# Sums of squares for the norm of k: the block of ones held in the array and the squares' exact halves streamed, 512 tokens at a time, then laid out through memory

## The chip, the cores and the metric

The kernel is one program on one core of one Trainium2 chip. A core has five engines that run at their own pace and wait for one another through semaphores: TensorE (PE in the rows; PEld is its weight load, which runs beside the matmul before it), VectorE (DVE), ScalarE (ACT), GpSimd (POOL) and SyncE (SP), which here only issues DMA transfers. Each engine takes its instructions strictly in the order in which they stand, DMA issues included (SPq and ACTq in the rows). A matmul has a stationary operand, loaded into the array first, and a moving operand that is streamed through it; its result goes to PSUM, and ACT or DVE copies it from there to SBUF.

The metric is the device time of the whole program in microseconds (us). Three runs of the kernel before took 3341.09, 3333.39 and 3338.21 us, so the median is 3338.21 us.

## The reference, cut to what matters

One layer of a bidirectional encoder: a combined projection, a bidirectional RWKV-7 scan (8 heads of 64, 2048 tokens), windowed attention, and a mixture of experts. The change touches one quantity, the norm of `kk` per head and token:

```python
k = u[..., 512:1024]                                  # columns of the projection, token-shifted
kk = heads(k * k_k)                                   # (2048 tokens, 8 heads, 64)
kk = kk / max(sqrt(sum(kk * kk, axis=-1)), 1e-12)     # one norm per head and token
...
wkv += wkv7_scan(r, decay, kd, v, -kk, kk * a, reverse)
```

So 8 x 2048 sums of 64 squares are wanted, and their inverse square roots are multiplied into `kk` before the scan reads it.

## The kernel before, in words

A scheduler orders the instructions of each engine when the program is built: the source is written stage by stage, and the scheduler interleaves what is ready by its own estimate of durations. The order is fixed from then on. Where a buffer (a named tile in a pool) is used again, the new user waits for the last reader of the old one; pools that are opened later take the same SBUF space as pools that were closed, and their first users wait for the last users of that space.

Four stages matter here.

**Norm and transposes (0 to about 72 us).** x is normalised and transposed into `hq[q]`, four quarters of 512 tokens each, as two parts whose sum is the exact value (`float32r`, a form that TensorE takes in one pass; plain float32 takes it two records of a matmul and of a weight load for each call).

**Projection in columns (about 37 to 397 us).** A loop takes 14 blocks `c` of 128 columns of w_in in the order 4, 5, 6, 7, 12, 13, 0, 1, 2, 3, 8, 9, 10, 11; blocks 4 to 7 are k, two heads each. For each block and each quarter, 24 matmuls (8 pieces of the inner dimension, 3 products of parts; L280) sum into one PSUM bank `pp` of 3, and ACT copies it to `u` (L283). So a block is 96 matmuls of 128x128 stationary and 512 moving columns. Then ACT scales `u` (L285) and DVE adds the two neighbour tokens (L286, L287) into `dst` (tile `m`, or `xwa` for block 12).

For a block of k, ACT squares `dst`, scaled by k_k, into `u` (L292), and 16 matmuls in plain float32 (L295) take 128 tokens each: the squares are stationary, `blk` (128x2, ones in the rows of one head per column) moves. Each leaves 128 tokens x 2 heads in one PSUM tile `ssq`, so tokens lie on partitions. After block 7, DVE takes the maximum with 1e-24 and the inverse square root (L316 and the helper at L104 to L109), PE transposes the result (L320), DVE copies it out (L322), and SP writes it to memory as `inv_d`, 8 heads x 2048 tokens (L323). From there ACT's queue reads it back, spread over 64 partitions (L265), in 16 pieces: `normalise` loads a piece of k (L262), multiplies (L267) and writes it (L268). The pieces are spread over blocks 13, 0, 1 and 2.

**Start of the scan (about 397 to 600 us).** SP loads 14 small parameter rows into `qrow` (buffer `Zs`, L346 to L350), the two up-projections `upw` (L353, L354), the v rows `uv` that blocks 8 to 11 wrote to memory (L304, L399) and the r, k, kk slices `ld` (L427). PE transposes `qrow` (L377). Then `prep` runs four times: matmuls (L436), tanh, a chain of DVE, ACT and POOL operations, transposes (L484), products (L493). `invert` follows, mainly on DVE, and then 64 steps of the scan.

**Filler.** The rest of the projection (attention columns and gates, "dense", L716 and L720; its weights come through L656, L658, L659) is a generator that is drawn in fixed numbers of steps between the pieces of `prep`, `invert` and the scan steps. The scheduler may move it further.

The lines that the sums rest on:

```python
S.activation(u[:, 0:T], dst, AF.Square, scale=P[:, 44 + pr:45 + pr])
for i in range(NT):
    o = ssq[:, :128].rearrange("p (h i) -> p h i", h=H)[:, 2 * pr:2 * pr + 2, i]
    PE.matmul(o, u[:, i * 128:(i + 1) * 128], blk, start=True, stop=True)
```

## Time and profile before

| | |
|---|---|
| runs | 3341.09, 3333.39, 3338.21 us; median 3338.21 us |
| the profiled execution's own time | 3351.28 us |
| its span, first to last instruction | 3349.6 us |
| PE busy | 3024.1 us, 90% of the span |
| DVE busy | 2210.9 us, 66% |
| ACT busy | 1522.0 us, 45% |
| mean granted TensorE clock | 0.957 of full speed |

How to read it. The profile comes from one execution. "Idle before" names what ended the idle time of an engine. A matmul's duration covers its whole way through the array, and the next one starts before it ends; what a matmul costs in a dense run is the distance from one start to the next, which is read from a stretch and its count. A `clock` of 1.00 is the level of 2.4 GHz and 0.50 that of 1.2 GHz; between them lies a stretch that had both.

### The profile page before, as it was taken

What the parts mean: (1) busy time and instruction counts of PE and PEld (TensorE: products, weight loads), DVE (VectorE), ACT (ScalarE), POOL (GpSimd) and SP (SyncE); (2) the same over time, 40 slices, a digit from 0 to 9 for tenths busy, and PEclk for the clock granted to TensorE, in tenths of its full rate; (3) what the DMA queues carried; (4) which work ended last, traced back from release to release, by engine and by line L of the source; (5) the groups of instructions that cost most, each with busy time, mean ns of one, the idle gap of its engine ahead of it and who ended that gap; (6) DMA issues with size and microseconds to landing.
All of it is one profiled execution on the core that took longest, in us unless ns stands there. A gap on an engine that the chain in (4) does not pass through costs nothing. (4 is left out here: it accounts for less than half of the span.)

```text
span 3349.6 us, 72079 instructions
## 1 busy us (share of the span) xinstructions
PE 3024.1 (90%) x29102; PEld 2466.8 (74%) x29102; DVE 2210.9 (66%) x4134; ACT 1522.0 (45%) x2913; POOL 544.8 (16%) x648
## 2 busy tenths in 40 slices
PE   6999978888989998898999987999996999999997
PEld 4888777667877787678877886778784667777775
DVE  5233368566766686648664776677774677888885
ACT  6333344453434434343433864111122566677764
POOL 0000012011112020112110000323233121222231
PEclk9899989999999999999999999999996999999999
DMA  7144365666545655565456654444433899999986
GB/s 280 60 136 137 98 208 194 211 199 206 161 150 174 201 167 160 166 199 162 145 172 184 182 174 144 129 130 144 127 120 115 286 308 323 337 336 341 330 295 201
DMA packets 361082, 652.63 MB, mean 195 GB/s; under 512 B 33717, under 2 KB 181765, under 8 KB 356522
## 3 DMA queue, kind: packets, MB, share of 16 engines
q1 hardware_dynamic: 338538, 599.61, 53.8%
q0 software_dynamic: 11104, 36.32, 4.4%
q10 hardware_dynamic: 11104, 12.06, 1.1%
q8 instruction: 230, 3.77, 0.5%
q14 instruction: 106, 0.87, 0.1%
HBM read 497.52 MB, written 153.10 MB: 194 GB/s over the span
## 5 line engine op out<-in xcount | busy, mean ns | idle before, releaser
L716 PE MATMUL dn<-wh,hk 128*128 128x256 f32 x3456 | 475.4, 295 | 24.0 <-DVE wh L659 9.4
L1289 DVE TENSOR_TENSOR wh<-raw,wh 128x1024 fp32r<-128x1024 f32 x376 | 441.4, 1219 | 80.1 <-ACT wh L1288 79.1
L716 PEld LDWEIGHTS dn<-wh,hk 128*128 128x128 f32 x3456 | 443.8, 200 | 42.5 <-DVE wh L659 11.1
L1288 ACT ACTIVATE wh<-raw 128x1024 fp32r<-128x1024 f32 x384 | 387.3, 1053 | 149.9 <-DMA raw<-in_w_down_dram 69.2
L720 PE MATMUL dn<-hk,wh 128*128 128x512 f32 x1536 | 404.1, 411 | 30.6 <-ACT gs L730 11.0
L1418 PE MATMUL pgu<-wh,xT 128*128 128x512 f32 x1536 | 377.7, 403 | 0.2 <-ACT xT L1393 0.2
L720 PEld LDWEIGHTS dn<-hk,wh 128*128 128x128 f32 x1536 | 284.5, 193 | 106.9 <-ACT gs L730 13.2
L1418 PEld LDWEIGHTS pgu<-wh,xT 128*128 128x128 f32 x1536 | 287.9, 190 | 78.1 <-issue 7.4
L280 PE MATMUL pp<-hq,wh 128*128 128x512 f32 x1008 | 254.0, 408 | 1.6 <-ACT hq L217 1.3
L280 PEld LDWEIGHTS pp<-hq,wh 128*128 128x128 f32 x1008 | 193.1, 194 | 48.0 <-ACT hq L217 2.3
L1174 PE MATMUL px<-w,mT 128*128 128x512 f32 x768 | 196.2, 406 | 0.0
L1462 PE MATMUL py<-wh,hT 128*128 128x512 f32 x768 | 191.4, 401 | 0.4 <-ACT hT L1440 0.4
L476 POOL TENSOR_TENSOR t<-t,ld 128x512 f32<-128x512 f32 x32 | 51.2, 1600 | 857.6 <-DVE t L465 483.9
L1174 PEld LDWEIGHTS px<-w,mT 128*128 128x128 f32 x768 | 142.8, 188 | 36.8 <-issue 3.4
L1462 PEld LDWEIGHTS py<-wh,hT 128*128 128x128 f32 x768 | 140.4, 188 | 33.1 <-issue 1.2
L1354 POOL DMA_INDIRECT out_dram<-ys,IDX x49 | 91.2, 1861 | 315.5 <-issue 105.5
L283 ACT ACTIVATE u<-pp 128x512 f32<-128x512 f32 x56 | 61.3, 1094 | 152.3 <-PE pp L280 125.3
L730 ACT ACTIVATE gs<-dn,drv 128x512 f32<-128x512 f32 x64 | 75.7, 1183 | 116.9 <-PE dn L720 80.5
L1158 PE MATMUL ab<-yT,w 128*128 128x256 f32 x768 | 114.4, 293 | 7.2 <-DVE tg L1161 3.6
L1378 POOL DMA_INDIRECT xg<-h_d,IDX x49 | 72.7, 1484 | 280.2 <-PE tx L1392 175.1
L1158 PEld LDWEIGHTS ab<-yT,w 128*128 128x128 f32 x768 | 99.5, 193 | 12.4 <-DVE tg L1161 5.6
L415 ACT ACTIVATE uv<-pre 32x512 f32<-32x512 f32 x128 | 75.2, 588 | 61.1 <-PE pre L409 59.9
(415 smaller groups left out, 5434.5 us busy)
## 6 DMA issues: line engine op xcount, KB each, us to landing
wh<-wc_d SPq DMA_DIRECT2D x204, 512.0 KB
raw<-in_w_gate_dram SPq DMA_DIRECT2D x64, 1024.0 KB
raw<-in_w_up_dram SPq DMA_DIRECT2D x64, 1024.0 KB
raw<-in_w_down_dram SPq DMA_DIRECT2D x64, 1024.0 KB
wc_d<-wh SPq DMA_DIRECT2D x68, 512.0 KB
ld<-rkk_d SPq DMA_DIRECT2D x192, 128.0 KB
raw<-in_w_in_dram SPq DMA_DIRECT2D x82, 256.0 KB
g_d<-gs SPq DMA_DIRECT2D x64, 256.0 KB
```

Of the source, the lines that this page charges most:

```text
L280: PE.matmul(pp, whs[k // 4][:, a, k % 4], hq[q][k // 2][:, k % 2, b], start=n == 0, stop=n == 3 * KT - 1)
L415: S.activation(uv[p * 64:p * 64 + 32, s::2].rearrange("p s (h e n) -> p s h e n", e=2, n=N)[:, :, :, e], pa[o:o + 32], AF.Copy)
L716: PE.matmul(pp[e][:, j * 256:(j + 1) * 256], lhs(2 * e + j, hk, k, a), wk_[:, b], start=k + j + m == 0, stop=k + j + m == KT + 2, skip_gro ...
L720: PE.matmul(pp[e], wk_[:, a, e * 128:e * 128 + 128], hk[k // 2][:, k % 2, b], start=k + m == 0, stop=k + m == KT + 1)
L730: S.activation(natural(gs), by_residue(pp[e]), AF.Tanh, scale=0.5, bias=DP[:, 38 + ct:39 + ct])
L1158: PE.matmul(pa[:, e], wt[k][:, a, cs_], src[:, k, b], start=e + n == 0, stop=n == 3 * nk - 1, skip_group_check=True)
L1174: PE.matmul(px, mT[k // 4][:, k % 4, a, j * 128:(j + 1) * 128], wO[k][:, b, fs], start=n == 0, stop=n == 3 * KT - 1)
L1288: S.activation(wh[:, 0, ks], raw[:, ks], AF.Copy)
L1289: eng.tensor_tensor(wh[:, 1, ks], raw[:, ks], wh[:, 0, ks], op=OP.subtract)
L1354: G.indirect_dma_start(out=x2_d, out_offset=bass.IndirectOffsetOnAxis(ap=idx, axis=0), in_=src, in_offset=None, bounds_check=T - 1, oob_is ...
L1418: PE.matmul(pgu[n], xT[:, x_, 4 * a + k], wh[:, w_, k], start=a + k + m == 0, stop=a + k + m == 6)
L1462: PE.matmul(py[f], hT[:, x_, 2 * a + k], wh[:, w_, k, f * 512:(f + 1) * 512], start=a + k + m == 0, stop=a + k + m == 4)
```

## The change

For each block of k, the squares in `u` are taken 512 tokens at a time. ACT copies them to `float32r` (the first half, `sh[:, 0]`), DVE subtracts that from the squares (the second half, `sh[:, 1]`; the two add up to the squares), and two matmuls sum both halves with `blkr`, the ones in `float32r`, as stationary operand (128x2): 2 partitions x 512 tokens in PSUM. ACT copies that to `sums` (2x2048), and SP writes `sums` to a new memory tensor `ss_d`, 8 x 2048. After block 7, SP reads `ss_d` back as 128 partitions x 128 tokens, DVE makes the inverse square roots in place of before, and SP writes them to `inv_d` as they lie; the transpose and the copy after it are gone. The pool `up` gets `blkr`, `sh` (two buffers of 4 KB a partition) and `sums` (8 KB), and loses `ivT`.

```diff
+    ss_d = scratch("ss_d", [H, T])
...
-        ssq = mk(ps1, [128, 512], F32, "ssq", bufs=1)
+        blkr = mk(up, [128, 2], F32R, "blkr")
+        S.activation(blkr, blk, AF.Copy)
...
                 S.activation(u[:, 0:T], dst, AF.Square, scale=P[:, 44 + pr:45 + pr])
-                for i in range(NT):
-                    o = ssq[:, :128].rearrange("p (h i) -> p h i", h=H)[:, 2 * pr:2 * pr + 2, i]
-                    PE.matmul(o, u[:, i * 128:(i + 1) * 128], blk, start=True, stop=True)
+
+                sums = mk(up, [2, T], F32, "sums")
+                for i4 in range(4):
+                    ts_ = slice(i4 * 512, (i4 + 1) * 512)
+                    sh = mk(up, [128, 2, 512], F32R, "sh", bufs=2)
+                    S.activation(sh[:, 0], u[:, ts_], AF.Copy)
+                    V.tensor_tensor(sh[:, 1], u[:, ts_], sh[:, 0], op=OP.subtract)
+                    pt = mk(ps1, [128, 512], F32, "ssq", bufs=1)
+                    for b in range(2):
+                        PE.matmul(pt[0:2], blkr, sh[:, b], start=b == 0, stop=b == 1)
+                    S.activation(sums[:, ts_], pt[0:2], AF.Copy)
+                nc.sync.dma_start(ss_d[2 * pr:2 * pr + 2], sums)
...
-                V.tensor_scalar(sv, ssq[:, :128], 1e-24, None, op0=OP.max)
+                nc.sync.dma_start(sv, ss_d.rearrange("h (i p) -> (h i) p", p=128))
+                V.tensor_scalar(sv, sv, 1e-24, None, op0=OP.max)
                 iv = mk(up, [128, 128], F32, "iv")
                 rsqrt(up, iv, sv, [128, 128], "rk")
-                pt = mk(ps1, [128, 512], F32, "tp")
-                PE.transpose(pt[:, :128], iv, ident)
-                ivT = mk(up, [128, 128], F32, "ivT")
-                V.tensor_copy(ivT, pt[:, :128])
-                nc.sync.dma_start(inv_d.rearrange("h (i p) -> (h i) p", p=128), ivT)
+                nc.sync.dma_start(inv_d.rearrange("h (i p) -> (h i) p", p=128), iv)
```

The scheduler's order changes at these places. From the projection's line on, lines of the kernel after stand 2 to 8 higher than those of before (L280 is now L282, L377 is L385, L436 is L444, L716 is L724).

PE before, in the second quarter of block 7 (`pp_1028`): the 16 matmuls for block 6's squares (`u_856`) stand in one piece.

```order
L280 MATMUL pp_1028<-hq_24_106,wh_152_996 128x512 x6
L280 MATMUL pp_1028<-hq_25_107,wh_152_996 128x512 x2
L295 MATMUL ssq_577<-blk_78,u_856 128x2 x16
L280 MATMUL pp_1028<-hq_25_107,wh_152_996 128x512 x4
L280 MATMUL pp_1054<-hq_26_108,wh_150_991 128x512 x6
```

PE after, the same place (second quarter `pp_1072`, third `pp_1098`): the eight matmuls for block 6 (L304) stand apart, a pair for each 512 tokens.

```order
L282 MATMUL pp_1072<-hq_26_108,wh_180_1040 128x512 x5
L304 MATMUL ssq_1003<-sh_1000,blkr_578 2x512
L282 MATMUL pp_1072<-hq_26_108,wh_180_1040 128x512
L282 MATMUL pp_1098<-hq_27_109,wh_178_1035 128x512
L304 MATMUL ssq_1003<-sh_1000,blkr_578 2x512
L282 MATMUL pp_1098<-hq_27_109,wh_178_1035 128x512 x4
L304 MATMUL ssq_1010<-sh_1007,blkr_578 2x512 x2
L282 MATMUL pp_1098<-hq_27_109,wh_178_1035 128x512
L282 MATMUL pp_1098<-hq_28_110,wh_178_1035 128x512 x3
L304 MATMUL ssq_1017<-sh_1014,blkr_578 2x512 x2
L282 MATMUL pp_1098<-hq_28_110,wh_178_1035 128x512 x3
```

Between two pairs stand four matmuls of the projection; the two of the first pair have two between them.

SP before, at the end of the projection: the 14 loads of `Zs` stand ahead of the last four stores of v (`v_d`); the two last of the 14 are the first two rows here.

```order
L349 DMA Zs_2626<-in_k_a_dram 8x64
L350 DMA Zs_2626<-in_r_k_dram 8x64
L427 DMA ld_2722<-rkk_d_58 64x4x128
L353 DMA upw_2642<-in_w_decay_up_dram 64x2x512
L304 DMA v_d_59<-vs_2586 128x4x128
L304 DMA v_d_59<-vs_2594 128x4x128
L354 DMA upw_2642<-in_a_gate_up_dram 64x2x512
L304 DMA v_d_59<-vs_2602 128x4x128
L304 DMA v_d_59<-vs_2610 128x4x128
L399 DMA uv_2704<-v_d_59 32x512 x3
L619 DMA gq_2699<-in_q_norm_g_dram 128x64
```

SP after, the same place: the 14 loads of `Zs` begin after the v stores and the first three loads of `uv` (its first four rows are the last here), and all six loads of `ld` come after them and the other loads of `uv`.

```order
L361 DMA upw_2697<-in_w_decay_up_dram 64x2x512
L315 DMA v_d_59<-vs_2641 128x4x128
L315 DMA v_d_59<-vs_2649 128x4x128
L362 DMA upw_2697<-in_a_gate_up_dram 64x2x512
L315 DMA v_d_59<-vs_2657 128x4x128
L315 DMA v_d_59<-vs_2665 128x4x128
L407 DMA uv_2759<-v_d_59 32x512 x3
L354 DMA Zs_2681<-in_w_decay_dram 4x64
L355 DMA Zs_2681<-in_a_gate_dram 4x64
L354 DMA Zs_2681<-in_w_decay_dram 4x64
L355 DMA Zs_2681<-in_a_gate_dram 4x64
```

The first load of `Zs` now also waits for the last two stores of v: its buffer lies in space that the larger pool `up` held.

PE before, where the scan begins: 28 filler matmuls stand between the last transposes of v (L301) and the transpose of `Zs` (L377), and 24 between the first `prep`'s L436 and its L484.

```order
L301 MATMUL tp_2605<-ident_70,m_2577 128x128 x4
L716 MATMUL dn_2851<-wh_350_2752,hk_101 128x256 x4
L716 MATMUL dn_2851<-wh_352_2758,hk_102 128x256 x12
L716 MATMUL dn_2851<-wh_354_2764,hk_103 128x256 x12
L377 MATMUL pre_2673<-ident_70,Zs_2626 128x40
L436 MATMUL pre_2731<-xwa_89,upw_2642 64x128 x8
L436 MATMUL pre_2799<-xwa_89,upw_2642 64x128 x8
L716 MATMUL dn_2979<-wh_358_2778,hk_100 128x256 x12
L716 MATMUL dn_3071<-wh_358_2778,hk_100 128x256 x12
L484 MATMUL pre_2966<-ident_70,bk_2897 128x128 x4
```

PE after, the same place:

```order
L724 MATMUL dn_2906<-wh_389_2819,hk_104 128x256 x12
L724 MATMUL dn_3034<-wh_393_2833,hk_101 128x256 x12
L724 MATMUL dn_3034<-wh_400_2922,hk_102 128x256 x12
L724 MATMUL dn_3034<-wh_402_2940,hk_103 128x256 x12
L724 MATMUL dn_3126<-wh_393_2833,hk_101 128x256 x12
L724 MATMUL dn_3126<-wh_400_2922,hk_102 128x256 x12
L724 MATMUL dn_3126<-wh_402_2940,hk_103 128x256 x12
L385 MATMUL pre_2728<-ident_71,Zs_2681 128x40
L444 MATMUL pre_2786<-xwa_90,upw_2697 64x128 x8
L444 MATMUL pre_2854<-xwa_90,upw_2697 64x128 x8
L492 MATMUL pre_3021<-ident_71,bk_2952 128x128 x4
```

There are now 100 filler matmuls ahead of the transpose of `Zs` and none between L444 and L492. The order of PE goes on differing through the four `prep`, `invert` and the first few scan steps, and is the same from there to the end.

## Rows read from the trace of the kernel before

**Rows 1.** The page: busy time of the engines over the span, and the granted clock in 40 slices of 84 us.

```profile
PE 3024.1 (90%) x29102; PEld 2466.8 (74%) x29102; DVE 2210.9 (66%) x4134; ACT 1522.0 (45%) x2913; POOL 544.8 (16%) x648
...
PEclk9899989999999999999999999999996999999999
```

**Rows 2.** Busy time in stretches: start and end, length, then each engine's busy us and instructions, granted clock, DMA share, GB/s.

```profile
92.00:176.00 84.00, 83.29 (x388) 69.48 (x389) 19.11 (x23) 26.68 (x23) 0.00 (x0) 0.90 0.19 66
176.00:330.00 154.00, 154.00 (x660) 124.48 (x659) 57.59 (x68) 56.46 (x52) 0.00 (x0) 0.99 0.43 139
330.00:380.00 50.00, 49.49 (x227) 39.54 (x226) 12.79 (x13) 19.06 (x22) 0.00 (x0) 1.00 0.31 95
412.00:437.00 25.00, 7.94 (x58) 7.09 (x59) 18.04 (x46) 9.65 (x25) 3.62 (x2) 0.55 0.52 155
540.00:600.00 60.00, 41.19 (x396) 36.27 (x395) 57.06 (x124) 20.61 (x45) 17.73 (x38) 0.83 0.42 146
```

**Rows 3.** PE alone, cut where a block's matmuls begin (the first from the second quarter of block 5): length, busy us (matmul records), granted clock, DMA share, GB/s. The first four hold 128 records of L295, 32 each; the last holds none.

```profile
79.86:103.70 23.84, 23.80 (x105) 0.86 0.30 113
103.70:131.60 27.90, 27.66 (x129) 0.94 0.16 57
131.60:161.07 29.47, 29.23 (x129) 0.88 0.15 54
161.07:189.05 27.98, 27.74 (x130) 0.94 0.19 69
189.05:211.33 22.28, 22.28 (x97) 1.00 0.43 130
```

**Rows 4.** PE alone, in stretches behind the L295 matmuls: columns as in Rows 3.

```profile
97.10:103.90 6.80, 6.80 (x23) 0.74 0.02 7
103.90:109.40 5.50, 5.50 (x25) 1.00 0.30 87
118.00:120.00 2.00, 2.00 (x6) 0.50 0.00 0
```

**Rows 5.** PE in order of time: start us, us, engine, line, operation, records, and in brackets the idle time before and what ended it.

```profile
137.07 4.83 PE L280 MATMUL pp<-hq,wh 128*128 128x512 f32 x20
142.14 4.35 PE L295 MATMUL ssq<-blk,u 128*128 128x2 f32 x32 [0.24 <-ACT u L292]
146.35 14.88 PE L280 MATMUL pp<-hq,wh 128*128 128x512 f32 x52
...
331.10 1.09 PE L301 MATMUL tp<-ident,m 128*128 128x128 f32 x8 [0.24 <-DVE m L287]
```

**Rows 6.** Groups of instructions from 60 to 410 us, shapes kept apart: busy us and mean ns of one, then the engine's idle time before them.

```profile
L295 PE MATMUL ssq<-blk,u 128*128 128x2 f32 x128 | 17.1, 269 | 0.8 <-ACT u L292 0.7
...
L137 DVE TENSOR_TENSOR wh<-raw,wh 128x512 fp32r<-128x512 f32 x24 | 16.6, 690 | 96.1 <-ACT wh L136 96.1
L136 ACT ACTIVATE wh<-raw 128x512 fp32r<-128x512 f32 x24 | 15.2, 632 | 26.7 <-PE pp L280 23.1 <-DMA vs<-rkk_d 3.5
```

**Rows 7.** The page's groups: an ACT copy out of PSUM of 32 partitions x 512.

```profile
L415 ACT ACTIVATE uv<-pre 32x512 f32<-32x512 f32 x128 | 75.2, 588 | 61.1 <-PE pre L409 59.9
```

**Rows 8.** All engines in order of time during block 7, whose PE work begins at 131.60.

```profile
137.27 1.10 ACT L283 ACTIVATE u<-pp 128x512 f32<-128x512 f32 x1 [2.06 <-PE pp L280]
137.63 2.35 DVE L287 SCALAR_TENSOR_TENSOR m<-u,prmT,m 128x2048 f32<-128x2048 f32 x1
...
140.08 2.01 ACT L292 ACTIVATE u<-m,prmT 128x2048 f32<-128x2048 f32 x1 [1.71 <-DVE m L287]
```

**Rows 9.** DMA issues of SP and ACT in order of time: the write of the inverse norms, the first read of them.

```profile
181.18 0.32 SPq L323 DMA_DIRECT2D inv_d<-ivT  x1
...
183.55 0.50 ACTq L265 DMA_DIRECT2D vs<-inv_d  x1
```

**Rows 10.** DMA issues of SP in order of time, at the end of the projection.

```profile
397.14 0.28 SPq L346 DMA_DIRECT2D Zs<-in_w_decay_dram  x1
...
401.79 0.29 SPq L350 DMA_DIRECT2D Zs<-in_r_k_dram  x1
...
411.69 1.04 SPq L304 DMA_DIRECT2D v_d<-vs  x2
412.82 1.51 SPq L399 DMA_DIRECT2D uv<-v_d  x3
415.08 0.36 SPq L619 DMA_DIRECT2D gq<-in_q_norm_g_dram  x1
...
415.97 6.00 SPq L399 DMA_DIRECT2D uv<-v_d  x13
422.01 3.23 SPq L427 DMA_DIRECT2D ld<-rkk_d  x5
```

**Rows 11.** PE in order of time, where the scan begins.

```profile
407.72 3.58 PE L716 MATMUL dn<-wh,hk 128*128 128x256 f32 x28
412.39 0.25 PE L377 MATMUL pre<-ident,Zs 40*128 40x40 f32 x1 [1.08 <-ACT vs L303]
...
416.43 2.93 PE L716 MATMUL dn<-wh,hk 128*128 128x256 f32 x12 [2.16 <-ACT qs L724]
420.79 2.93 PE L716 MATMUL dn<-wh,hk 128*128 128x256 f32 x12 [1.43 <-ACT qs L724]
436.79 1.94 PE L484 MATMUL pre<-ident,bk 128*128 128x128 f32 x8 [13.08 <-DVE bk L477]
```

## The prediction

> **What bounds the kernel now.** I read the page first: PE is busy for 90% of the span, and its clock is at the upper level in most slices [rows 1]. The chain of waits that ends last says nothing on a change in the first tenth, so I went by stretches. In the projection PE has no pause: 154.00 of 154.00 us from 176 to 330, and 83.29 of 84.00 from 92 to 176, while DVE and ACT have 19 and 27 us to do there [rows 2]. So in this stage the length of PE's own work is the time, and ACT and DVE have room. Only the stretch with the k blocks shows a clock under 1: 0.90 [rows 2].
>
> Next I cut PE's time where blocks begin [rows 3]. A block of 96 matmuls without sums of squares takes 22.28 us, so one matmul costs 22.28 / 96 = 0.232 us. The four stretches that hold the sums take 23.84 (72 matmuls, for which 16.71 are due), 27.90, 29.47 and 27.98. Their excess is 7.13 + 5.62 + 7.19 + 5.70 = 25.6 us. That is all that this part of the kernel costs. It has three pieces: 17.1 us of L295 [rows 6], 0.7 us of waits for ACT's squares [rows 6], and some 7.5 to 7.8 us left over. The remainder is the clock: behind L295 it is granted at 0.50 or 0.74, that is at 1.2 GHz for much of the stretch, and is back at 1.00 six or seven us later [rows 4]; 52 matmuls take 14.88 us there [rows 5] instead of 12.1.
>
> **What goes.** The 128 records of L295, and with them the excess: 25.6 us. The transpose L320 lies inside it. That the clock stays up without L295 I take from the matmuls of the projection, which alone hold it at 1.00 in the block after [rows 3].
>
> **What PE gets.** 4 blocks x 4 pieces x 2 halves = 32 matmuls with 512 moving columns in float32r. The same form with 128 stationary columns costs 0.232 us; a stationary operand of 2 columns is not in the trace, but the weight load of 128 is hidden there already. 32 x 0.232 = 7.4 us. Bounds: 512 columns at 2.4 GHz are 0.213 us, 6.8 in all; twice 0.232 if all ran at the lower clock, 14.9. I take 7.4.
>
> **What PE waits for.** The eight matmuls of a block stand in the stream in pairs with four projection matmuls, 0.93 us, between them, and whatever a pair waits for, all projection matmuls behind it wait too. From block 7's start at 131.60, as the rows have it: ACT's squares end at 142.09 [rows 8], the first copy at 142.09 + 0.63 = 142.72 [rows 6]. PE has 47 matmuls ahead of it, 131.60 + 10.91 = 142.51, and waits 0.2. The second half needs DVE's subtraction, 0.69 more [rows 6], 143.41; PE has done two projection matmuls by 143.42: no wait. Then ACT has the second copy and the 1.10 us copy of the quarter [rows 8], which it can start when the 24th matmul is out, about 143.3, so the copy of the first sums begins at 144.4 and ends at 145.0, by the 0.588 of an ACT copy of 32x512 out of PSUM [rows 7]. The PSUM bank `ssq` has one buffer: the second pair may start at 145.0, and PE is there after 143.65 + 0.93 = 144.6: 0.4. Later pairs have no quarter to wait for; copy, handover and the next copy fit in about 0.93 + 0.46, so I give them nothing. Sum 0.2 + 0.4 = 0.6 a block, 2.6 us for four with a little rounding up. Below, it is 0. Above, if copy, subtraction, the pair and the copy out ran one after the other for each piece, 0.63 + 0.69 + 0.46 + 0.59 = 2.4 less 0.93 of cover would be a wait of 1.4 to 1.6 us with the handovers, 16 times 22 to 26 us.
>
> ACT gets 4 x (0.63 + 0.59) = 4.9 us a block, DVE 4 x 0.69 = 2.8. They have 27 and 19 us of work in the 84 us [rows 2]; PE's stream hides it except for the waits above.
>
> **The path through memory.** `ss_d` is written and read back before the inverse roots, two transfers that cost about 0.32 + 2.05 us each, as from the write of `inv_d` at 181.18 to its first reader at 183.55 [rows 9]. More: the last step of the roots now stands on DVE behind block 12's two token additions, so `inv_d` is written when these are done, which is 8.4 us into the next block (139.98 - 131.60 [rows 8]) instead of 8 us ahead of it. About 8.4 + 2.4 = 10.8 us into block 13, and one short DVE step later, it can be read. Behind that read on ACT's queue stands the copy of the second quarter, whose matmuls are done at 0.232 x 48 = 11.1 us; three banks `pp` give PE another 11 us. No cost. On SP the weights of block 1 stand behind the wait, two blocks ahead of their use. `normalise` ends some 17 us later than before against the rest, with the blocks 3 and 8 to 11 still ahead of the scan. No cost either.
>
> So the projection ends 25.6 - 7.4 - 2.6 = 15.6 us sooner.
>
> **The start of the scan.** All times here are those of before, to which the 15.6 us are a common shift. The loads of `Zs` wait for the last stores of v. `gq` waits for the same stores now and is issued at 415.08 [rows 10], so `Zs` starts there; 14 issues at (401.79 - 397.14) / 13 = 0.36 us [rows 10] and 2.05 for landing [rows 9] give 422.1, against 412.39 for the transpose [rows 11]: 9.7 us late. PE is covered: 100 filler matmuls at 3.58 / 28 = 0.128 us [rows 11] keep it busy from 407.72 to 420.5. Then nothing covers the first `prep`. Its loads `ld` land at about 420.1 + 0.8 (`gq`) + 6.0 (`uv`) + 3.9 (six `ld`) + 2.05 = 432.9 [rows 10], and five DVE operations of 0.69 on them give 436.4 for the transposes L484, which before start at 436.79 behind 13.08 us of idleness [rows 11]. So they come at the same time, with 48 more filler matmuls done by then, 48 x 0.128 = 6.1 us. Whether that is a gain depends on the stretch from 540 to 600, where DVE is busy for 57.06 of 60 us and PE for 41.19 [rows 2]: filler that is done sooner is missing there. I take 0, the row of that stretch being nearest, with -6.1 and +9.7 as ends (the latter if the whole chain moves with the transpose of `Zs`). From the first scan steps on, the order is the same and the shift is carried to the end.
>
> **Sum.** 3351.28 us of the profiled execution less 15.6 is 3335.7. That execution was 13 us over the median of the runs; the saving is in work, so I take it from the median: 3338.2 - 15.6 = 3322.6, about 3323 us.
>
> **Rivals.**
>
> *The clock does not come back.* If the pairs and the short waits for `ssq` let the clock fall as L295 does, the 7.5 us stay: 15.6 - 7.5 = 8.1, 3330 us. Against it: PE waits 0.24 us and then does short transposes at 331.10 [rows 5], and the stretch from 330 to 380 is at 1.00 [rows 2]; for it: nothing shows what a 2-column stationary operand does. The Trainium skill speaks against the change here: its page "TensorE: Matmul & The Clock Gate" (A second HAM failure mode: psum-queue depth-cycling) tells of a kernel that cycled through PSUM banks, paused briefly between groups, and had its clock swing between both levels. The rows from 330 to 380 show no such swing for pauses of 0.24 us; by that rule the result would be this rival.
>
> *The scan starts late.* All 9.7 us of the late `Zs` stay: 15.6 - 9.7 = 5.9, 3332 us. For it: the chain through `prep` to the scan steps is one after the other, and PE stood idle for 17 of 25 us in it [rows 2]. Against it: `ld` and five DVE operations, not the tanh, are last.
>
> *Slower: the pieces run one after the other.* The single `ssq` bank and the order on ACT make each of 16 pieces wait 1.6 us: 25.6 - 7.4 - 25.6 = -7.4, 3346 us. It decides from (25.6 - 7.4) / 16 = 1.14 us a piece. Against it: the copies and subtractions of the next piece are independent of the bank and stand ahead on ACT and DVE.
>
> **How the numbers follow.** Forecast 0.66 (3323; its own range 3313 to 3330: no waits and 6 us at the scan, or waits twice as long and half the clock loss), clock 0.11, late scan 0.13, slower 0.06, something else 0.04. The three runs of before spread by 8 us. Range 3310 to 3334. About 0.2%, 6.7 us, is what a measurement here can tell from no change, so the bound for faster is 3331.5: forecast 0.64, clock 0.07, late scan 0.06, else 0.01, together 0.78; within 0.2% 0.15; slower 0.07.
>
> **What would show it.** Right: the blocks 5, 6, 7 and 12 take about 22.3 + 1.9 + 0.6 = 24.8 us each at a clock of 1.00; the new matmuls sit 0.232 us apart; the idle time ahead of the second pair in a block is under half a us; the projection's last matmul is some 15 us sooner. L385 waits one or two us for a DMA, and L492 13 to 15 us for DVE. Wrong: a clock under 1 between 92 and 176, PE waiting over 1 us for ACT's `sums` at each piece, or PE standing still for clearly more than the 17 us of [rows 2] between the end of the projection and the first L492.

## The result, and the profile after

The kernel after takes 3316.28 us (median of five runs, 3312.55 to 3319.97) beside 3338.21 us for before: a ratio of 0.9925 (0.9908 to 0.9942). Two more comparisons of the same kernel, below, gave 0.9924 and 0.9935; weighted by their intervals the three give 0.9928 (0.9916 to 0.9940), about 24 us. The forecast was 3323 us.

The profiled execution took 3319.97 us. Two lines of the page answer to [rows 1]; PE's busy time falls by 14 us, while ACT and DVE have more to do:

```profile
PE 3009.8 (91%) x29005; PEld 2449.2 (74%) x29005; DVE 2219.4 (67%) x4149; ACT 1538.3 (46%) x2946; POOL 563.3 (17%) x648
...
PEclk9999988999989999999999998999997999999998
```

The stretch with the k blocks, as in [rows 2] (length, then busy us and instructions of PE, PEld, DVE, ACT, POOL, granted clock, DMA share, GB/s). The clock is 1.00 where it was 0.90, and the ACT and DVE work that was added is there, under a PE that is still busy for 82.49 of 84 us:

```profile
92.00:176.00 84.00, 82.49 (x352) 61.39 (x352) 31.14 (x43) 48.93 (x61) 0.00 (x0) 1.00 0.21 76
```

The blocks themselves, cut as in [rows 3]: first from the second quarter of block 5 on (PE alone), then blocks 6, 7 and 12 (all engines), then block 13 without sums (PE alone):

```profile
80.85:100.05 19.20, 18.85 (x81) 1.00 0.40 147
...
100.05:124.90 24.85, 24.45 (x106) 18.44 (x105) 8.66 (x10) 13.95 (x17) 0.00 (x0) 1.00 0.16 58
124.90:149.76 24.86, 24.47 (x106) 18.44 (x105) 8.84 (x10) 13.70 (x16) 0.00 (x0) 1.00 0.18 65
149.76:174.60 24.84, 24.47 (x105) 18.44 (x104) 9.94 (x15) 13.71 (x16) 0.00 (x0) 1.00 0.19 68
...
174.60:196.87 22.27, 22.27 (x98) 1.00 0.24 74
```

The four stretches with sums take 19.20, 24.85, 24.86 and 24.84 us, where before they took 23.84, 27.90, 29.47 and 27.98: 15.44 us less. At the projection's end the gain is all there: the 28 filler matmuls right behind the last transposes of v start at 393.21 in place of 407.72, 14.5 us sooner; that is one us less than 15.44 because this execution reached block 5 one us later (80.85 against 79.86).

PE in order of time in block 6, with the matmuls of block 5's sums (L304):

```profile
105.49 5.53 PE L282 MATMUL pp<-hq,wh 128*128 128x512 f32 x23
111.25 0.40 PE L304 MATMUL ssq<-sh,blkr 128*2 128x512 f32 x1 [0.22 <-ACT sh L300]
111.48 0.62 PE L282 MATMUL pp<-hq,wh 128*128 128x512 f32 x2
111.97 0.39 PE L304 MATMUL ssq<-sh,blkr 128*2 128x512 f32 x1
112.20 1.10 PE L282 MATMUL pp<-hq,wh 128*128 128x512 f32 x4
113.47 0.63 PE L304 MATMUL ssq<-sh,blkr 128*2 128x512 f32 x2 [0.18 <-ACT sums L305]
113.94 1.10 PE L282 MATMUL pp<-hq,wh 128*128 128x512 f32 x4
114.88 0.63 PE L304 MATMUL ssq<-sh,blkr 128*2 128x512 f32 x2
```

Read it by starts. A matmul of the sums is followed 0.23 us later by the next one, as forecast. Two waits are named, 0.22 for the first copy and 0.18 for the bank. Each costs more than its bracket says: the four matmuls from 112.20 on are due by 112.20 + 4 x 0.232 = 113.13, and the next one starts at 113.47, so 0.34 us are lost where 0.18 is shown, since the tail of the matmul before the wait still counts as busy (one takes 0.39 to 0.40 us by its record, and the next starts 0.23 us after it). For the first wait it is 0.4 us where 0.22 is shown.

Behind the projection, where the scan begins (PE, as in [rows 11]):

```profile
393.21 3.59 PE L724 MATMUL dn<-wh,hk 128*128 128x256 f32 x28
400.42 11.14 PE L724 MATMUL dn<-wh,hk 128*128 128x256 f32 x72 [3.62 <-ACT qs L732]
411.50 0.25 PE L385 MATMUL pre<-ident,Zs 40*128 40x40 f32 x1
427.38 1.94 PE L492 MATMUL pre<-ident,bk 128*128 128x128 f32 x8 [13.96 <-DVE bk L485]
```

The transpose of `Zs` (L385) waits for nothing; it stands behind a wait of 3.62 us for ACT. L492 is 9.4 us sooner than L484 was, not 14.5, with 48 more filler matmuls done by then.

So 15.4 of some 22 to 24 us are seen in the rows of the projection. The experiments ask two things: what in the old sums cost so much, and whether the rest has a place.

### The profile page after: what moved, and what is told of

The parts are those of the page before. It is cut to its first block, busy times and chain, and to the rows that moved or that the text cites. A ratio compares the mean times of both kernels' runs of the same rounds, so it can differ in the third digit from the quotient of the medians.

```text
span 3318.2 us, 71986 instructions
## 1 busy us (share of the span) xinstructions
PE 3009.8 (91%) x29005; PEld 2449.2 (74%) x29005; DVE 2219.4 (67%) x4149; ACT 1538.3 (46%) x2946; POOL 563.3 (17%) x648
## 5 line engine op out<-in xcount | busy, mean ns | idle before, releaser
L724 PE MATMUL dn<-wh,hk 128*128 128x256 f32 x3456 | 472.4, 294 | 19.3 <-DVE wh L667 5.5
L724 PEld LDWEIGHTS dn<-wh,hk 128*128 128x128 f32 x3456 | 441.0, 198 | 38.5 <-issue 10.6
L282 PE MATMUL pp<-hq,wh 128*128 128x512 f32 x1008 | 248.7, 399 | 1.4 <-ACT hq L218 1.1
L282 PEld LDWEIGHTS pp<-hq,wh 128*128 128x128 f32 x1008 | 188.1, 189 | 47.1 <-ACT hq L218 1.8
L484 POOL TENSOR_TENSOR t<-t,ld 128x512 f32<-128x512 f32 x32 | 53.7, 1677 | 806.9 <-DVE t L473 525.3
L1362 POOL DMA_INDIRECT out_dram<-ys,IDX x49 | 102.5, 2092 | 303.7 <-issue 93.9
```

The costliest lines, as they stand in the source:

```text
L282: PE.matmul(pp, whs[k // 4][:, a, k % 4], hq[q][k // 2][:, k % 2, b], start=n == 0, stop=n == 3 * KT - 1)
L724: PE.matmul(pp[e][:, j * 256:(j + 1) * 256], lhs(2 * e + j, hk, k, a), wk_[:, b], start=k + j + m == 0, stop=k + j + m == KT + 2, skip_gro ...
L1362: G.indirect_dma_start(out=x2_d, out_offset=bass.IndirectOffsetOnAxis(ap=idx, axis=0), in_=src, in_offset=None, bounds_check=T - 1, oob_is ...
```

## The experiments

Each kernel was compared with before on the same chip. `space`, `spread`, `plain`, `narrow` and the other variants share one order of PE with after, from 100 instructions ahead of L385 to the end (`own` and `again` have that of before). Where the text speaks of the four stretches it means the blocks 5, 6, 7 and 12 whole, which take 115.45 us in before (73.60 to 189.05) and 100.00 in after.

**The kernel before once more.** No edit.

> The kernel before, unchanged, once more. It gives a second profile of it and the size of a difference that means nothing. Main theory: the projection of before costs 25.6 us more than its plain matmuls in any execution, while the 31 us between the two profiled spans hold about 10 us that have nothing to do with the change; so here the four k stretches again take 23.8, 27.9, 29.5 and 28.0 us, the span differs from the first profile's 3349.6 by some 5 to 15 us behind the projection, and the ratio to before is 1.000 within 0.0015. Rival: the profiled 31 us are all the change's, and this profile has the span of the first one, 3349 to 3350 us.

Ratio 0.9989 (0.9978 to 0.9999), span 3346.9 us, stretches of 27.88, 29.46 and 27.98 us for the blocks 6, 7 and 12:

```profile
103.59:131.47 27.88, 27.64 (x129) 22.69 (x128) 6.18 (x6) 9.31 (x8) 0.00 (x0) 0.94 0.16 57
131.47:160.93 29.46, 29.23 (x129) 23.91 (x128) 6.18 (x6) 9.34 (x8) 0.00 (x0) 0.88 0.15 54
```

The blocks of the projection repeat to 0.02 us; the whole does not. A kernel against itself was off by 0.0011, at the edge of its interval, so single ratios of this study are good to two or three parts in a thousand, and lengths in the projection to a tenth of a microsecond. The span differed from the first profile by 2.7 us, less than the 5 to 15 expected.

**Only the start of the scan.** Tiles as large as the new ones are reserved in `up`, and nothing reads them:

```diff
...
+                sums = mk(up, [2, T - 128], F32, "sums")
+                V.memset(sums[:, 0:1], 0.0)
+                for i4 in range(4):
+                    sh = mk(up, [128, 2, 512], F32R, "sh", bufs=2)
+                    V.tensor_copy(sh[:, 0, 0:2], blk)
                 for i in range(NT):
                     o = ssq[:, :128]...
```

> The kernel before with its own sums of squares, but with tiles of the size of blkr, sh and sums reserved in the pool up (written in a few elements, read by nobody). By that the order of PE behind the projection is the one of the kernel after. It tells what the start of the scan brings by itself. Theory S6: the 48 more filler matmuls that are done by the first transposes of prep are kept to the end, 48 x 0.128 = 6.1 us, so about 3332 us, a ratio of 0.998. Theory S0 (the value of the prediction): nothing, 3338 us, 1.000. Theory S10: the late loads of Zs and ld cost 9.7 us, 3348 us, 1.003. In all three the k stretches stay at 27.9, 29.5 and 28.0 us with a clock of 0.90 from 92 to 176.

Ratio 0.9997 (0.9984 to 1.001), so -5.3 to +3.3 us. The rows show the order of after at work, the same 13.96 us ahead of the transposes of `bk`, and the clock of before:

```profile
92.00:176.00 84.00, 83.27 (x392) 69.08 (x391) 18.72 (x19) 28.06 (x24) 0.00 (x0) 0.91 0.20 72
...
417.36 11.55 PE L723 MATMUL dn<-wh,hk 128*128 128x256 f32 x72 [4.72 <-ACT qs L731]
444.72 1.94 PE L491 MATMUL pre<-ident,bk 128*128 128x128 f32 x8 [13.96 <-DVE bk L484]
```

S0 holds; S10 lies outside the interval, and S6, at 0.998 against its lower end of 0.9984, only just. The rows agree with S0: by the end of the scan nothing is left of the filler that was done sooner, for the scan's last matmul from L580 (L587 in this kernel) starts 1403 us behind the last projection matmul in both kernels (396.7 to 1799.9 in before, 398.1 to 1801.4 here).

**What lowered the clock: short records, or their type?** `plain` streams 512 columns in plain float32, without halves:

```diff
...
-                    for b in range(2):
-                        PE.matmul(pt[0:2], blkr, sh[:, b], start=b == 0, stop=b == 1)
+                    PE.matmul(pt[0:2], blk, u[:, ts_], start=True, stop=True)
```

> The kernel after without the split: the squares move in plain float32 against the ones in plain float32, 16 calls of 512 columns, each two records; the copies into sh, the subtractions and the second half are gone. Theory A, only the records count, and the clock stays up when 512 columns move: by the 0.43 us from record to record that plain float32 matmuls of 128x512 have in the trace of before, 16 x 2 x 0.43 = 13.8 us in place of 7.4, so 6 us slower than after, some 3322 us, blocks of k about 25.8 us long at a clock of 1.00. Theory B, it is the plain float32 form that lowered the clock behind L295: the clock from 92 to 176 falls to about 0.9 again, blocks of 27 to 28 us, 3329 us or more.

Ratio 0.9944 (0.9929 to 0.9959), blocks of 27.15 us, and the clock stays up:

```profile
102.35:129.49 27.14, 26.90 (x105) 18.06 (x104) 6.16 (x6) 11.53 (x12) 0.00 (x0) 1.00 0.14 52
...
112.88 1.02 PE L298 MATMUL ssq<-u,blk 128*2 128x512 f32 x2 [0.24 <-ACT u L292]
113.83 1.19 PE L280 MATMUL pp<-hq,wh 128*128 128x512 f32 x4
114.95 1.02 PE L298 MATMUL ssq<-u,blk 128*2 128x512 f32 x2
```

Plain float32 does not take the clock down by itself: theory A. But the price was too low: a call takes 0.95 us (112.88 to 113.83), 0.475 a record and not 0.43, and the four projection matmuls behind it take 1.12 in place of 0.93. So the split in halves is worth 27.15 - 24.85 = 2.3 us a block, for all its copies and subtractions. And 27.15 - 22.27 = 4.9 us a block are no less than the old records cost where the clock stays up (4.5, below): what `plain` gains in the blocks over before is the clock alone.

`narrow` keeps the old layout, with the halves in float32r and four moving columns, the ones twice over:

```diff
-                    PE.matmul(o, u[:, i * 128:(i + 1) * 128], blk, start=True, stop=True)
...
+                        for b in range(2):
+                            PE.matmul(o, sh[:, b, i % 4 * 128:i % 4 * 128 + 128], blkr, start=b == 0, stop=b == 1)
```

> The kernel before with its layout (128 tokens of squares stationary, the ones moving, tokens on partitions of the result, no way through memory), but with the squares' halves and the ones in float32r, and four moving columns, the ones twice over: 128 records of 128x4 in place of 128 records of 128x2 in plain float32. The order behind the projection is that of after. Theory A, records that move a few columns lower the clock whatever their type: the clock from 92 to 176 stays near 0.90, the k blocks take 27 us or more, and the time is that of the kernel space, or up to 5 us less. Theory B, plain float32 lowered the clock: it stays at 1.00, the 128 records cost what their loads take, 128 x 0.06 to 0.08 = 8 to 10 us, blocks of about 24.5 us, and the time is that of after, 3316 to 3320 us.

Ratio 0.9978 (0.9966 to 0.9989). Of the blocks three keep the clock (26.28 us for block 6) and one, block 7, loses it:

```profile
100.82:127.10 26.28, 26.08 (x130) 21.51 (x128) 8.84 (x10) 11.74 (x12) 0.00 (x0) 1.00 0.14 51
127.10:158.13 31.03, 30.84 (x129) 25.49 (x128) 8.84 (x10) 11.77 (x12) 0.00 (x0) 0.83 0.14 51
...
112.92 0.95 PE L304 MATMUL ssq<-blkr,sh 128*128 128x4 f32 x8
113.73 0.71 PE L283 MATMUL pp<-hq,wh 128*128 128x512 f32 x2
```

Neither theory as it stood: float32r loses the clock too, but in one block of four. It is no pause of PE that holds it down there: from 141.30 to 151.50 PE is busy for 10.20 of 10.20 us at 0.50. The records cost 0.101 us each at the upper level (eight from 112.92 to 113.73) and not 0.06 to 0.08, 13 us for 128, against 7.4 for the 32 of after. This kernel also differs from before in the grouping, so:

**The same plain records in groups of eight.** `space` with ACT's squares in four pieces:

```diff
-                S.activation(u[:, 0:T], dst, AF.Square, scale=P[:, 44 + pr:45 + pr])
+                for i4 in range(4):
+                    ts_ = slice(i4 * 512, (i4 + 1) * 512)
+                    S.activation(u[:, ts_], dst[:, ts_], AF.Square, scale=P[:, 44 + pr:45 + pr])
```

> The kernel space (sums as before, order behind the projection as after) with ACT's squares in four pieces of 512 tokens, so that the plain float32 records of L295, 128x2 as before, stand in groups of 8 with projection matmuls between them, in place of 32 in one piece. In the kernel narrow, groups of 8 records of 128x4 in float32r took the clock down in one block of four, to 0.94 on the mean; in before 32 plain float32 records in one piece took it down in all four. Theory A, the length of one piece of short records decides: the clock from 92 to 176 is 0.94 or more and at most two blocks of four show 0.50. Theory B, the type decides: every block still shows it, mean 0.90, blocks of 27.9 to 29.5 us.

Ratio 1.0015 (0.9998 to 1.0032). Blocks 5, 6, 7 and 12, the first from 74.00 on:

```profile
74.00:101.51 27.51, 27.36 (x135) 22.03 (x135) 14.08 (x54) 11.81 (x14) 0.00 (x0) 1.00 0.49 183
101.51:132.69 31.18, 30.83 (x129) 25.52 (x128) 6.18 (x6) 9.88 (x11) 0.00 (x0) 0.84 0.14 51
132.69:160.70 28.01, 27.66 (x129) 22.77 (x128) 6.18 (x6) 9.88 (x11) 0.00 (x0) 0.94 0.16 57
160.70:187.48 26.78, 26.42 (x130) 21.52 (x129) 10.45 (x20) 9.88 (x11) 0.00 (x0) 1.00 0.20 72
```

Two of four blocks keep the clock, where none does in before: nearer to theory A, with 0.92 from 92 to 176 in place of the 0.94 it asked for. So it is streams of short records, of either type, that risk the clock; splitting them helps in some blocks and not in others, at 28.0 and 31.2 us for the two blocks that fall here and 26.8 for the last one, which doesn't. Why one group of eight takes the clock down and the next does not, the runs don't show; nor do they part the few moving columns from the stationary operand of 128 columns that each of these records brings, since every kernel with long records holds the two columns of ones. The last block also gives an estimate of the price of L295 without its clock loss: 26.78 - 22.27 = 4.5 us, 18 for four, so that some 25.6 - 18 = 7.6 us of before were clock. No kernel with 512 moving columns showed a clock under 1.00 there.

**What the new sums still cost.** `twice` runs each matmul of the sums twice, so that the sums come out doubled; `nosum` runs none and leaves k without its norm:

```diff
-                    for b in range(2):
-                        PE.matmul(pt[0:2], blkr, sh[:, b], start=b == 0, stop=b == 1)
+                    for b in range(4):
+                        PE.matmul(pt[0:2], blkr, sh[:, b % 2], start=b == 0, stop=b == 3)
```

```diff
-                        PE.matmul(pt[0:2], blkr, sh[:, b], start=b == 0, stop=b == 1)
-                    S.activation(sums[:, ts_], pt[0:2], AF.Copy)
+                    S.activation(sums[:, ts_], sh[0:2, 0], AF.Copy, scale=0.0, bias=64.0)
```

> The kernel after with each of the 32 matmuls of the sums done twice into the same bank (the sums come out doubled, so k's norm is off by the root of 2). Theory: 32 more matmuls of 0.23 us, 7.4 us, blocks of k of 24.85 + 1.86 = 26.7 us at a clock of 1.00, so 7 us over after. Rival, the wait for the bank grows with its use (it is held longer, so the copy out comes later): 0.46 us more at each of the 16 pieces, some 7 us on top, blocks of 28 us or more. Rival, the stationary operand of two columns takes the clock down when there are more of them: clock under 1 between 92 and 176.

> The kernel after without the 32 matmuls of the sums and their bank: ACT writes a constant to sums in place of the copy out of PSUM, so k is not normalised. The floor: what the sums still cost. Theory: the blocks of k fall to 22.3 us, 4 x 2.58 = 10.3 us less than after, of which 7.4 are matmuls, about 1.5 waits and the rest gaps around them; ratio to before 0.9923 if only the projection counts, 0.989 to 0.990 if after keeps a gain behind the projection. Rival: copies on ACT still hold PE up, and blocks stay at 23 us or more.

`twice`: 0.9968 (0.9952 to 0.9984), blocks of 26.35 us at a clock of 1.00. `nosum`: 0.9929 (0.9903 to 0.9955), blocks of 22.27. The rows of `twice` show the four matmuls of a piece and no wait for the bank between pieces:

```profile
112.75 0.85 PE L304 MATMUL ssq<-sh,blkr 128*2 128x512 f32 x3
113.44 1.10 PE L282 MATMUL pp<-hq,wh 128*128 128x512 f32 x4
114.37 1.09 PE L304 MATMUL ssq<-sh,blkr 128*2 128x512 f32 x4
```

So a block of after is 22.27 + 1.86 for eight matmuls + 0.72 of waits = 24.85. Doubling adds 1.50 and not 1.86; the 0.36 between them are about the wait for the bank (0.34 by starts in after), which the rows of `twice` no longer have. Both rivals of `twice` fall, and so does that of `nosum`.

**The pieces one after the other.** `sh1` has one buffer for the halves. `own` puts halves and sums into buffers that `up` had before, by which it has the order of before behind the projection:

```diff
-                    sh = mk(up, [128, 2, 512], F32R, "sh", bufs=2)
+                    sh = mk(up, [128, 2, 512], F32R, "sh", bufs=1)
```

```diff
-                sums = mk(up, [2, T], F32, "sums")
+                sums = u[0:2, 0:T]
...
-                    sh = mk(up, [128, 2, 512], F32R, "sh", bufs=2)
+                    sh = [mk(up, [128, 512], F32R, "vs", bufs=2) for _ in range(2)]
```

> The kernel after with one buffer for the halves (sh) in place of two, so that the copy of the next 512 squares waits until both matmuls on the last ones are done: the rival in which the pieces run one after the other, made on purpose. Theory: copy 0.62, subtraction 0.7, the pair 0.46 to 0.6 and the handovers make a cycle of about 2.0 to 2.3 us against 1.4 us of PE work per piece, so PE waits 0.6 to 0.9 us at three of four pieces, 2 to 3 us a block, blocks of 27 to 27.5 us and 8 to 11 us over after. Rival: the order built for it puts more projection matmuls between the pairs, and blocks stay under 25.5 us.

> The kernel after with its new sums, but in the space that before had in the pool up: the halves go into the two buffers vs, the sums into u. By that the order of PE from the scan's start to the end is that of before. Against sh1, which has the same one-piece-at-a-time handover in the projection, it tells what the other order is worth when the projection is short. Theory O0: nothing, as in the kernel space; it differs from before by what its four k stretches are shorter. Theory O10: the excess of after over its 15.45 us of projection, 6 to 10 us, comes from the order, and is gone here, while sh1 has it.

`sh1`: 0.9940 (0.9920 to 0.9959), blocks of 24.75 to 24.93 us, its rival. The order that was built for it spreads the matmuls, two of the projection between halves and six between pieces, and it keeps PE from waiting for the bank at all; what is left are 1.2 us of waits for ACT's copies into `sh`, where after has 1.0 and 0.5 for the bank. PE in `sh1`, then the groups of `sh1` and of after:

```profile
111.67 0.40 PE L304 MATMUL ssq<-sh,blkr 128*2 128x512 f32 x1
111.90 1.55 PE L282 MATMUL pp<-hq,wh 128*128 128x512 f32 x6
113.30 0.40 PE L304 MATMUL ssq<-sh,blkr 128*2 128x512 f32 x1
...
L304 PE MATMUL ssq<-sh,blkr 128*2 128x512 f32 x32 | 12.6, 392 | 1.2 <-ACT sh L300 1.2
```

```profile
L304 PE MATMUL ssq<-sh,blkr 128*2 128x512 f32 x32 | 10.7, 394 | 1.5 <-ACT sh L300 1.0 <-ACT sums L305 0.5
```

`own`: 0.9954 (0.9939 to 0.9969). Its four stretches are 15.07 us shorter than before's, which alone gives 0.9955. Both theories asked for that; what parts them is `sh1`, which has the order of after and should gain 6 to 10 us beside its stretches by O10. Its 0.9940 is 4 us below the 0.9952 of its stretches, an interval that holds both nothing and 10 us. So these two kernels don't decide; what speaks against O10 are the other kernels with the order of after, taken together further below. With the order of before the wait ahead of L492 is 13.08 us again, as in [rows 11]:

```profile
396.79 0.25 PE L385 MATMUL pre<-ident,Zs 40*128 40x40 f32 x1 [0.49 <-ACT vs L314]
421.20 1.94 PE L492 MATMUL pre<-ident,bk 128*128 128x128 f32 x8 [13.08 <-DVE bk L485]
```

**One half, two banks.** A form with still less to do; the low half of the squares is left out of the sums:

```diff
-                    V.tensor_tensor(sh[:, 1], u[:, ts_], sh[:, 0], op=OP.subtract)
-                    pt = mk(ps1, [128, 512], F32, "ssq", bufs=1)
-                    for b in range(2):
-                        PE.matmul(pt[0:2], blkr, sh[:, b], start=b == 0, stop=b == 1)
+                    pt = mk(psq, [128, 512], F32, "ssq", bufs=2)
+                    PE.matmul(pt[0:2], blkr, sh[:, 0], start=True, stop=True)
```

> The kernel after with only the first half of the squares in float32r (one matmul per 512 tokens, no subtraction; the rounded-off rest of the squares is left out of the sums) and two banks for ssq. Theory: 16 matmuls of 0.232 us less, 3.7 us, and the waits for the bank go, 0.2 a block; blocks of 22.27 + 0.93 + 0.2 to 0.4 = 23.4 to 23.6 us, the projection 5 to 6 us shorter than in after, the ratio 0.001 to 0.002 lower. Rival: PE reaches each piece sooner and waits for ACT's copies instead, so that blocks stay above 24.2 us.

Blocks of 23.63 us, as expected, and the four stretches 4.5 us shorter than in after (95.49 us in place of 100.00). The ratio, 0.9952 (0.9935 to 0.9970), does not show it: it was to come out 0.001 to 0.002 lower than that of after, and lies higher (3329.42 us beside the 3319.50 of `after_third`, against the same runs of before). A gain of this size is below what these comparisons can tell.

**The kernel after, twice more.**

> The kernel after, unchanged, beside more runs of before. In the first comparison it gained 0.75% (0.58 to 0.92), some 22 us at the medians, while its four k stretches are only 15.45 us shorter in the traces, and the kernel space showed that the other order at the scan's start brings nothing. Theory P, the projection is all: ratio 0.9954, and the first comparison's excess was chance, since the clock behind the projection differs from run to run. Theory E, something behind the projection gains as well: ratio 0.992 to 0.993 again.

> The kernel after, unchanged, a third time, for its interval. Theory P, the projection's 15.45 us are all: 0.9954. Theory E, the result holds a gain behind the projection too: 0.9925, as twice before. With the two earlier comparisons this puts the mean's interval at about 0.0013 to each side.

0.9924 (0.9894 to 0.9954) and 0.9935 (0.9915 to 0.9956), with stretches 15.47 and 15.44 us shorter than before's. By the interval of the three together, 0.9916 to 0.9940, it is theory E; but that interval knows only the scatter from run to run, and the table below shows that kernels lie off their stretches by 0.0037 below to 0.0022 above, so the excess of after is not shown to be its own.

What the four stretches give against what was measured (us from the traces, over 3340; then the ratio):

| kernel | four stretches, us | ratio by them | measured |
|---|---|---|---|
| again | 0.0 | 1.0000 | 0.9989 |
| space | 0.0 | 1.0000 | 0.9997 |
| spread | -2.4 | 0.9993 | 1.0015 |
| narrow | -4.1 | 0.9988 | 0.9978 |
| plain | -6.3 | 0.9981 | 0.9944 |
| twice | -9.1 | 0.9973 | 0.9968 |
| own | -15.1 | 0.9955 | 0.9954 |
| after, three times | -15.45 | 0.9954 | 0.9925, 0.9924, 0.9935 |
| sh1 | -16.0 | 0.9952 | 0.9940 |
| lean | -20.0 | 0.9940 | 0.9952 |
| nosum | -25.6 | 0.9923 | 0.9929 |

## Why the prediction was right, and where it was not

*What goes.* Right. All 25.6 us of excess were the sums': without them the blocks fall to 22.27 us (`nosum`). Its parts hold too, by the estimate from one block of `spread`: 18 us of L295 and its waits, 7.6 us of clock, where 17.8 and 7.5 to 7.8 were put down. That the clock stays up without L295 is shown by every kernel with 512 moving columns. The rival "the clock does not come back" falls: after pauses at `ssq` in three blocks, and the clock is 1.00. The rule named beside it, from the Trainium skill, page "TensorE: Matmul & The Clock Gate" (A second HAM failure mode: psum-queue depth-cycling), does not describe this case: two pauses a block, of 0.4 and 0.34 us from start to start, left the clock at 1.00. What swung here were streams of short matmuls.

*What PE gets.* Right: 0.23 us from start to start with a stationary operand of two columns.

*What PE waits for.* Right in place and nearly in size: 0.6 us a block were forecast, 0.72 measured as 24.85 - 22.27 - 1.86. The wait for the first copy was twice the 0.2 that was put down, 0.4 us; the one for the bank was 0.34 for 0.4, and no other wait counts. Together with the matmuls 10.2 us against 10.0, so the projection's gain was 15.4 for 15.6.

*The path through memory.* Right. `inv_d` is written 8.7 us into block 13 and its first read is issued 10.2 us into it, where 8.4 and 10.8 were forecast, and block 13 takes 22.27 us:

```profile
183.29 0.32 SPq L331 DMA_DIRECT2D inv_d<-iv  x1
...
184.84 0.50 ACTq L267 DMA_DIRECT2D vs<-inv_d  x1
```

*The start of the scan.* The value, nothing, was right (`space`), but its working was wrong, and so luck had a part in it. It had `ld` and five DVE operations last, and L492 at the same time as before against the common shift. L492 came 5 us late. The 100 filler matmuls contain a wait of 3.62 us for ACT's `qs` and run partly at the lower clock (0.50 from 398.8 to 405.6), so L385 starts at 411.50, 3.9 us later than forecast against the shift of 14.46, and waits for no DMA at all, though one or two us were expected. From there the tanh and the DVE chain take 15.9 us to L492, longer than `ld` does: DVE's last idle time is for ACT, until 421.54, and the last of the six issues of `ld` ends at 416.02. In before `ld` was not last either. DVE had the filler's norm (L671 to L686) to do between L465 and its first step on `ld`, and in after part of that norm is done ahead of L385 and the rest before ACT's `cs` is there; so L385 to L492 takes 15.9 us where L377 to L484 took 24.4. DVE in after, then in before:

```profile
421.54 0.43 DVE L473 TENSOR_SCALAR t<-t 128x512 f32<-128x512 f32 x1 [2.89 <-ACT cs L472]
421.88 0.68 DVE L487 TENSOR_TENSOR ar<-ld,t 128x512 f32<-128x512 f32 x1
```

```profile
422.44 0.43 DVE L465 TENSOR_SCALAR t<-t 128x512 f32<-128x512 f32 x1 [4.13 <-ACT cs L464]
...
432.37 0.68 DVE L479 TENSOR_TENSOR ar<-ld,t 128x512 f32<-128x512 f32 x1
```

The end of the scan need not feel the late L492. In `space` it stands 46.6 us behind the last projection matmul where before has 40.1, and yet both reach the scan's end after 1403 us; that the filler done sooner is what makes up for it is argued from these lengths and not shown by itself.

*The rival that ended slower*, pieces one after the other, falls in its price: in after the wait for the bank is 0.34 us once a block. Even with one buffer (`sh1`) the handovers cost no more, since the order is built around the buffers and puts more projection matmuls between the pieces.

*The sum.* 3323 forecast, 3316 measured, inside the likeliest case's own range. The step that stays short is the last one, that the projection's shift is carried to the end and no more: after gains 24 us (20 to 28) by its three ratios, 15.4 of them in the projection. The other 5 to 13 have no place that the runs could settle. The order behind the projection does not make them by itself: `space` has it and gains nothing, `twice`, `nosum` and `lean` have it with the path through memory, and keep to their stretches within their intervals. `plain` has an excess like that of after. From the last projection matmul to the last L588 (L580 in before) the three profiles of after take 1391, 1399 and 1395 us, those of before 1403 and 1400, and `lean`, with the same instructions in the same order, 1406. The spread among kernels is as large as what is to be explained, so it stays open.

Part of that spread goes with the clock granted behind the projection. Executions of one and the same kernel already do so: of the 29 of before that stand beside `own` and `lean`, the shortest took 3330.90 us at a mean clock of 0.960, the longest 3355.70 at 0.954. And from the last matmul of that line of the scan to the end, where PE's order is the same in all, `plain` takes 1536.6 us at 0.970, before 1549.6 at 0.964 and `twice` 1552.2 at 0.961 in the profiled executions; the 13 us between `plain` and before are as much as `plain`'s whole excess. For after this does not do: its three profiles take 1545 to 1549 us there at 0.962 to 0.964, much as before does. What makes the clock differ there from one execution to the next, no run shows.

## What to carry to other kernels

A small reduction on TensorE is priced by what it does to the dense stream around it: count the excess of a block over the same block without it, and split it in records, waits and clock. Stream the long side and hold the ones: 32 matmuls of 512 columns in float32r cost less than 128 of two to four, and the clock stays up, even though ACT and DVE get more work. In plain float32 the same turn saves nothing but the clock (`plain`). Before believing a ratio of a few parts in a thousand, compare the kernel with itself, look at the clock that the executions were granted, and let the lengths of the stretch in the trace decide.

## What was not expected

A wait between pipelined matmuls costs about twice what its bracket shows (0.34 for 0.18). Plain float32 matmuls of 512 columns cost 0.475 us a record amid float32r ones, and the four float32r matmuls behind a pair take 1.12 us in place of 0.93. And the same group of eight short records took the clock to 0.50 in some blocks and left it at 1.00 in others of one execution (`spread`, `narrow`).
